# Merging three attention groups four heads at a time instead of eight

## The chip, the cores and the metric

The kernel runs on one core of a Trainium2 chip. The core has TensorE (PE in the profile: matrix multiply, with PEld for its weight loads), VectorE (DVE), ScalarE (ACT), GpSimd (POOL) and SyncE (SP), whose instruction stream issues all the transfers of this kernel. Each engine runs its own instructions in order, and engines wait for each other by semaphores. The metric is the device time of one execution in microseconds; of the kernel before there are three runs, 1656.64, 1657.37 and 1660.12 us.

## The reference

A trunk of two layers on 1024 tokens of width 1024. Layer A mixes tokens by dilated windowed attention, layer B by windowed attention with grouped keys. After each there is a residual layer norm and a gated addition. The part that matters here is in layer A: three groups of projections, each with its own window and dilation, and 16 heads of 64. Each group gives an output and a log-sum-exp per token and head, and the three are merged by a softmax over the groups:

```python
for gi, (window, dil) in enumerate(A_GROUPS):          # ((128, 1), (512, 4), (2048, 16))
    q, k, v = split_cols(h[..., base:base + 3 * A_WIDTH], [A_WIDTH] * 3)
    ...
    o, lse = banded_attention(strided(q)[:, :, :, None, :], strided(k), strided(v), window // dil)
    ...
wts = jax.nn.softmax(jnp.stack(lses, axis=0), axis=0)
o = jnp.einsum('gbsh,gbshd->bshd', wts, jnp.stack(outs, axis=0))
return (o * jax.nn.silu(z)) @ w_out
```

## The kernel before

Every projection is done with operands split into a high and a low half-precision part, so that one tile of 128 tokens by 512 columns is three matmuls for each of eight slices of the width, 24 in all (`lin`, L266 to L276). Weights come in blocks of 512 columns. A block is loaded in four transfers (`wraw`), its maximum is found by four VectorE reductions (L109), spread over the partitions by one small matmul on PE (`max_spread`, L237, which waits for VectorE's `mdd`), and it is split by ScalarE (L132) and VectorE (L133). These steps are handed out a few to a tile, ahead of the block's use.

Layer A (L623) runs over two pairs of four-head quarters (`pair`, and `q` from 0 to 3). For each pair and each group `g` in the order 1, 2, 0 there is a value stage of eight token tiles (v of the pair, L649 to L652) and two query/key stages (q and k of one quarter, L661 to L668). A query/key tile goes through the rotary step on VectorE (L347, L350), GpSimd (L351, L358) and ScalarE (L357, L361) and a transposing transfer (`qk`, L362). 1.67 tiles later (`UNIT_LAG`) an attention unit of four heads is due: scores on PE (L385), masked maximum on VectorE (L389), exponentials on ScalarE (L395), split of the weights (L399, L401), a transposing transfer (`pT`, L404); three units later the product with v on PE (L416 to L418), into one of two halves of a PSUM bank, which ScalarE empties into `st` (L698). `st` holds 256 output columns and 8 numbers for the denominators, and is stored to a DRAM tensor `scr` of its group (L707). Group 0 is the last, so when its tile is stored for both quarters of a pair, the three groups of that tile can be merged.

That is `merge`, a generator in three steps, which `merge_step` drives: at every third tile during most of the layer, at every tile from the second pair's group 0 on (`merge_every`). Step one loads the three groups from `scr` into `gt` (L749); step two computes the weights on VectorE with one exponential on ScalarE (L754 to L762) and starts the sum on GpSimd (L765 to L767); step three ends it on VectorE (L769, L770) and stores to `o_dr` (L771; `oa` in the profile). Two merges are under way at a time, in two buffers.

Behind layer A stands the gate projection `z`: eight tiles of its first half and one of the second in `z_block` (each through two ScalarE activations, L720 and L722, and VectorE's L723, and a store to `za`), the other seven in `mixed`. There each row tile's merged output `ot` and gate `og` are loaded, multiplied on GpSimd (L902), measured and split (L904, L263, L264) and transposed to `ogT`, from which the output projection reads (L920). One of its two weight blocks (`wo`) lies in a pool which is opened only when layer A's buffers are given back.

The source gives an order of creation, and a scheduler that models the engines in time moves instructions on each engine from it, so the order on an engine is read from the built program.

## Time and profile before

| what | value |
|---|---|
| median of three runs | 1657.37 us |
| the profiled execution | 1658.17 us, of which the span is 1656.4 us |
| PE busy | 1587.8 us, 96% of the span |
| VectorE, ScalarE, GpSimd busy | 1078.1, 922.7, 664.6 us |
| merges | 16, of eight heads and 128 tokens each |

The span is the time from the first to the last instruction that the profiler recorded on the core; the 1.8 us around it belong to the execution and are in no row. A busy PE is not yet PE at its peak, because the granted clock has two levels, 1.2 and 2.4 GHz, and a stage at the lower one is busy as well. The profile's column PEclk gives the mean of what was granted in a stretch as a share of 2.4 GHz. Idle time of another engine costs nothing as long as PE does not wait for it.

### The profile page before, as it was taken

The page shows a single profiled execution, that of the slowest core. Times are in us where ns is not written, and L with a number is a line of the kernel's source. Part 1 is how long each engine was busy: PE and PEld are TensorE (multiplying, and loading weights), DVE is VectorE, ACT ScalarE, POOL GpSimd, SP SyncE. Part 2 cuts the span into 40 slices and gives each one's busy share as a digit, 9 for nine tenths or more (in the row PEclk, how much of TensorE's full clock was granted, in tenths as well). Part 3 has the DMA queues.
Part 4 walks back from the last instruction along what each step waited for, and adds up shares of the span by engine and source line. Part 5 has one row for each costly group of instructions (what it writes and reads, how often), then busy time and mean ns, then how long its engine had stood idle before and what let it go on. Part 6 is the DMA issues. An engine that isn't in the chain of part 4 may idle for free. (4 is left out here: it accounts for less than half of the span.)

```text
span 1656.4 us, 29029 instructions
## 1 busy us (share of the span) xinstructions
PE 1587.8 (96%) x10579; PEld 883.2 (53%) x10579; DVE 1078.1 (65%) x2619; ACT 922.7 (56%) x2050; POOL 664.6 (40%) x477
## 2 busy tenths in 40 slices
PE   9999999999999799999999988899999998999998
PEld 3455676654555456666545543344455555544444
DVE  6866655655566776556466567887447998677731
ACT  4537665675774467656657843533334878754321
POOL 0015624532554665155235653453323452225341
PEclk9999999999999999999999998999999999999999
DMA  9718867775887777567658885989975898998963
GB/s 362 251 61 172 186 135 149 153 158 126 164 159 203 207 170 159 127 157 163 142 124 187 190 226 202 336 221 264 248 185 113 155 206 183 189 297 215 262 197 109
DMA packets 543792, 311.02 MB, mean 188 GB/s; under 512 B 473120, under 2 KB 494240, under 8 KB 543392
## 3 DMA queue, kind: packets, MB, share of 16 engines
q1 hardware_dynamic: 543648, 309.16, 75.3%
q8 instruction: 83, 1.36, 0.3%
q14 instruction: 61, 0.50, 0.1%
HBM read 137.78 MB, written 54.92 MB: 116 GB/s over the span
## 5 line engine op out<-in xcount | busy, mean ns | idle before, releaser
L272 PE MATMUL lin<-whl,xhl 128*128 128x512 f16 x1280 | 488.5, 382 | 2.6 <-ACT zu L722 2.6
L273 PE MATMUL lin<-whl,xhl 128*128 128x512 f16 x1280 | 488.7, 382 | 0.0
L274 PE MATMUL lin<-whl,xhl 128*128 128x512 f16 x1280 | 488.7, 382 | 0.0
L351 POOL TENSOR_TENSOR t<-t,t 128x512 f32<-128x512 f32 (+1 forms) x120 | 153.4, 1278 | 284.8 <-DVE t L350 268.0
L401 POOL TENSOR_TENSOR phl<-sm,phl 128x1024 f16<-128x1024 f32 (+1 forms) x88 | 155.6, 1769 | 233.3 <-ACT phl L399 205.9
L109 DVE TENSOR_REDUCE wpm<-wraw 128x1 f32<-128x1024 f32 (+1 forms) x132 | 156.8, 1197 | 93.6 <-DMA wraw<-in_wa_dram 54.8
L274 PEld LDWEIGHTS <-xhl 128*128 128x128 f16 x1280 | 149.3, 117 | 127.5 <-issue 3.5
L273 PEld LDWEIGHTS <-xhl 128*128 128x128 f16 x1280 | 149.7, 117 | 119.5 <-issue 6.7
L272 PEld LDWEIGHTS <-xhl 128*128 128x128 f16 x1280 | 149.4, 117 | 119.7 <-issue 3.8
L395 ACT ACTIVATE sm<-sm,st,cs 128x128 f32<-128x128 f32 (+1 forms) x384 | 203.6, 532 | 3.6 <-ACT st L393 0.4
L358 POOL TENSOR_TENSOR hl<-t,hl 128x512 f16<-128x512 f32 (+1 forms) x120 | 145.3, 1211 | 131.7 <-ACT hl L357 131.7
L389 DVE CUSTOM_DVE_ANT_0 sm<-s,tab 128x256 f32<-128x256 f32 (+1 forms) x512 | 157.0, 358 | 31.5 <-PE s L385 23.0
L133 DVE SCALAR_TENSOR_TENSOR whl<-wraw,s,whl 128x1024 f16<-128x1024 f32 (+1 forms) x116 | 168.3, 1501 | 12.8 <-ACT whl L132 12.8
L357 ACT ACTIVATE hl<-t 128x512 f16<-128x512 f32 (+1 forms) x120 | 72.3, 602 | 125.4 <-POOL t L351 124.0
L347 DVE TENSOR_TENSOR t<-lin,rope 128x512 f32<-128x512 f32 (+1 forms) x120 | 78.9, 657 | 75.7 <-PE lin L274 41.6
L132 ACT ACTIVATE whl<-wraw,s 128x1024 f16<-128x1024 f32 (+1 forms) x116 | 121.8, 1122 | 5.1 <-DVE s L212 5.0
L272 PE MATMUL lin<-whl,x2T 128*128 128x512 f16 (+1 forms) x320 | 115.5, 361 | 0.0
L273 PE MATMUL lin<-whl,x2T 128*128 128x512 f16 (+1 forms) x320 | 115.2, 360 | 0.0
L274 PE MATMUL lin<-whl,x2T 128*128 128x512 f16 (+1 forms) x320 | 115.0, 359 | 0.0
L399 ACT ACTIVATE phl<-sm 128x1024 f16<-128x1024 f32 (+1 forms) x128 | 110.2, 861 | 1.2
L361 ACT ACTIVATE hl<-hl 128x512 f16<-128x512 f16 (+1 forms) x104 | 63.2, 608 | 54.2 <-POOL hl L358 53.9
L385 PE MATMUL s<-qk 128*128 128x128 f16 x1120 | 81.5, 220 | 9.1 <-DMA qk<-hl 9.1
(187 smaller groups left out, 2883.5 us busy)
## 6 DMA issues: line engine op xcount, KB each, us to landing
wraw<-in_wa_dram SPq DMA_DIRECT2D x56, 512.0 KB, 6.0
scr<-st SPq DMA_DIRECT2D x96, 132.0 KB, 2.3
gt<-scr SPq DMA_DIRECT2D x48, 264.0 KB, 3.4
wraw<-in_wav_dram SPq DMA_DIRECT2D x24, 512.0 KB, 6.4
prh<-pro SPq DMA_DIRECT2D x32, 256.0 KB, 4.1
wraw<-in_wg_dram SPq DMA_DIRECT2D x16, 512.0 KB, 8.7
wraw<-in_wb_dram SPq DMA_DIRECT2D x16, 512.0 KB, 6.4
xg<-y SPq DMA_DIRECT2D x16, 512.0 KB, 3.6
```

The costliest lines, as they stand in the source:

```text
L109: k.nc.vector.tensor_reduce(pm[:, c:c + 1], self.raw[:, c * q:(c + 1) * q], axis=AX.X, op=ALU.max, apply_absolute_value=True)
L132: nc.scalar.activation(hl[:, 0, sl], self.raw[:, sl], AF.Copy, scale=self.s)
L133: self.last = nc.vector.scalar_tensor_tensor(hl[:, 1, sl], self.raw[:, sl], self.s, hl[:, 0, sl], op0=ALU.mult, op1=ALU.subtract)
L272: mm(ps, xh(kt), wh, start=(kt == 0), stop=False)
L273: mm(ps, xh(kt), wl, start=False, stop=False)
L274: mm(ps, xl(kt), wh, start=False, stop=(kt == NK - 1))
L351: nc.gpsimd.tensor_add(t1[:, :nh * HD], t1[:, :nh * HD], t2[:, :nh * HD])
L358: nc.gpsimd.tensor_sub(hl[:, :nh, HD:P], rv, hl[:, :nh, 0:HD])
L389: nc.vector.tensor_tensor_reduce(sm[:, h, :nk], ps[:, i, :nk], mask, 1.0, -3e38, ALU.add, ALU.max, mx[:, h:h + 1])
L395: nc.scalar.activation(sm[:, h, :nk], sm[:, h, :nk], AF.Exp, bias=nbias[:, h:h + 1], scale=cs, accum_out=sums[:, h:h + 1])
L399: nc.scalar.activation(hl[:, 0], sm[:, :, :nk], AF.Copy)
L401: eng.tensor_sub(hl[:, 1], sm[:, :, :nk], hl[:, 0])
```

## The change

A merge now covers one quarter, that is four heads, instead of a pair of quarters. It is created whenever a tile of group 0 is stored, for each `q`, and not only for the second of a pair. Its buffer `gt` holds half as many columns, there are three such buffers instead of two, and `merge_step` keeps up to three merges under way. All operations of a merge stay, on half as many elements; there are 32 merges.

```diff
-            if g == 0 and q % 2:
-                self.merges.append(self.merge(n, q // 2, scr[q // 2]))
+            if g == 0:
+                self.merges.append(self.merge(n, q, scr[q // 2]))
...
-    def merge(self, n, pair, scr):
+    def merge(self, n, q, scr):
...
-        gt = at.tile([P, 3, 2, 4 * HD + 8], F32, tag="gt", name="gt")
+        gt = at.tile([P, 3, 4 * HD + 8], F32, tag="gt", name="gt", bufs=3)
         for g in range(3):
-            nc.sync.dma_start(gt[:, g], scr[g][n * P:(n + 1) * P])
-        sums, nb = gt[:, :, :, 4 * HD:4 * HD + 4], gt[:, :, :, 4 * HD + 4:]
+            nc.sync.dma_start(gt[:, g], scr[g][n * P:(n + 1) * P, q % 2])
+        sums, nb = gt[:, :, 4 * HD:4 * HD + 4], gt[:, :, 4 * HD + 4:]
         yield
-        w = sp.tile([P, 3, 2, 4], F32, tag="mw", name="mw")
-        M = sp.tile([P, 2, 4], F32, tag="mM", name="mM")
...
+        w = sp.tile([P, 3, 4], F32, tag="mw", name="mw", bufs=3)
+        M = sp.tile([P, 4], F32, tag="mM", name="mM")
...
         nc.scalar.activation(w, w, AF.Exp)
...
         nc.gpsimd.tensor_mul(x[1], x[1], wb[1])
         nc.gpsimd.tensor_mul(x[2], x[2], wb[2])
         nc.gpsimd.tensor_add(x[1], x[1], x[2])
         yield
         nc.vector.tensor_mul(x[0], x[0], wb[0])
         nc.vector.tensor_add(x[0], x[0], x[1])
-        nc.sync.dma_start(self.o_dr[n][:, pair * 512:(pair + 1) * 512].rearrange("p (a c) -> p a c", a=2),
-                          gt[:, 0, :, 0:4 * HD])
+        nc.sync.dma_start(self.o_dr[n][:, 4 * HD * q:4 * HD * (q + 1)], gt[:, 0, 0:4 * HD])
...
-        while len(self.merging) < 2 and self.merges:
+        while len(self.merging) < 3 and self.merges:
```

The instructions move with it. VectorE, late in the z tiles, before: `zu` is a z tile (here the tenth and eleventh), `gt` belongs to the last two merges, `wpm` is the maximum of the first gate weight block.

```order
L109 TENSOR_REDUCE wpm_11795<-wraw_11693 128x1
L762 TENSOR_TENSOR mw_11620<-mw_11620,mL_11627 128x24
L723 SCALAR_TENSOR_TENSOR zu_11683<-zt_11681,zu_11683 128x512
L769 TENSOR_TENSOR gt_11610<-gt_11610,mw_11620 128x2x256
L109 TENSOR_REDUCE wpm_11795<-wraw_11693 128x1
L770 TENSOR_TENSOR gt_11559<-gt_11559 128x2x256
L109 TENSOR_REDUCE wpm_11795<-wraw_11693 128x1 x2
L239 TENSOR_REDUCE m2_11744<-s_11742 128x1
L770 TENSOR_TENSOR gt_11610<-gt_11610 128x2x256
L723 SCALAR_TENSOR_TENSOR zu_11728<-zt_11726,zu_11728 128x512
L218 TENSOR_REDUCE m1_11831<-wpm_11795 128x1
```

The same place on VectorE now, from the end of the last merge on (the first `zu` is the eighth z tile, the next the ninth and tenth):

```order
L769 TENSOR_TENSOR gt_11835<-gt_11835,mw_11881 128x256
L770 TENSOR_TENSOR gt_11835<-gt_11835 128x256
L723 SCALAR_TENSOR_TENSOR zu_11930<-zt_11928,zu_11930 128x512
L133 SCALAR_TENSOR_TENSOR whl_11970<-wraw_10759,s98_11899,whl_11970 128x1024 x4
L723 SCALAR_TENSOR_TENSOR zu_11966<-zt_11964,zu_11966 128x512
L109 TENSOR_REDUCE wpm_12131<-wraw_12029 128x1 x2
L723 SCALAR_TENSOR_TENSOR zu_12019<-zt_12017,zu_12019 128x512
L109 TENSOR_REDUCE wpm_12131<-wraw_12029 128x1 x2
L239 TENSOR_REDUCE m2_12080<-s_12078 128x1
L218 TENSOR_REDUCE m1_12167<-wpm_12131 128x1
```

The last merge operation (L770) stood between the tenth and the eleventh z tile, among the maxima (L109) of the next block; now it stands ahead of the eighth, and the split of a block (L133) and the maxima follow without a merge between them.

PE, where the output projection begins, before: L237 is the small matmul that spreads the maximum of the second gate weight block, `ogT` the first row tile.

```order
L274 MATMUL lin<-whl,xhl 128x512
L237 LDWEIGHTS ones
L237 MATMUL s<-mdd,ones 128x128
L272 LDWEIGHTS ogT
L272 MATMUL lin<-whl,ogT 128x512
L273 LDWEIGHTS ogT
```

The same matmul on PE now:

```order
L274 MATMUL lin<-whl,ogT 128x512
L237 LDWEIGHTS ones
L237 MATMUL s<-mdd,ones 128x128
L272 LDWEIGHTS ogT
L272 MATMUL lin<-wo,ogT 128x512
L273 LDWEIGHTS ogT
```

It stood between the last z tile and the first projection from `ogT`; now it stands 120 matmuls later, between the two halves of the third row tile.

SP's queue in the last query/key stage (second pair, group 0, `q` = 3), before. `scr0_1` to `scr2_1` are the three groups' stores of the second pair.

```order
L362 DMA_TRANSPOSE qk_10221<-hl_10227 128x12x128
L404 DMA_TRANSPOSE pT_10287<-phl_10284 128x16x128
L707 DMA scr0_1_618<-st_10050 128x264
L362 DMA_TRANSPOSE qk_10322<-hl_10328 128x12x128
L404 DMA_TRANSPOSE pT_10388<-phl_10385 128x16x128
L707 DMA scr0_1_618<-st_10154 128x264
L404 DMA_TRANSPOSE pT_10479<-phl_10476 128x8x128
L362 DMA_TRANSPOSE qk_10421<-hl_10427 128x12x128
L707 DMA scr0_1_618<-st_10254 128x264
```

The same stage on SP now, about the same transposes:

```order
L362 DMA_TRANSPOSE qk_10189<-hl_10195 128x12x128
L404 DMA_TRANSPOSE pT_10255<-phl_10252 128x16x128
L707 DMA scr0_1_618<-st_9998 128x264
L362 DMA_TRANSPOSE qk_10311<-hl_10317 128x12x128
L749 DMA gt_10400<-scr0_1_618 128x264
L771 DMA oa0_599<-gt_10152 128x256
L707 DMA scr0_1_618<-st_10100 128x264
L404 DMA_TRANSPOSE pT_10377<-phl_10374 128x16x128
L749 DMA gt_10521<-scr0_1_618 128x264
L749 DMA gt_10521<-scr1_1_619 128x264
L749 DMA gt_10521<-scr2_1_620 128x264
```

Between the transposes of `qk` and `pT` there are now three loads and a store of a merge to each tile. The exponentials of the first pair stood all in the value stage behind it and in the stage after that; now seven of the 16 stand in the query/key stage of `q` = 1. The second pair's eight for `q` = 2 stand in that of `q` = 3.

## Rows read from the trace of the kernel before

**Rows 1.** The page: busy us (share of the span) and instructions of each engine

```profile
PE 1587.8 (96%) x10579; PEld 883.2 (53%) x10579; DVE 1078.1 (65%) x2619; ACT 922.7 (56%) x2050; POOL 664.6 (40%) x477
```

**Rows 2.** Stage windows: stretch, length, busy us (count) per engine, PEclk, DMA share, GB/s

```profile
core 0: us, PE busy (x) PEld busy (x) DVE busy (x) ACT busy (x) POOL busy (x), PEclk, DMA share, GB/s
420.00:508.00 88.00, 88.00 (x715) 49.55 (x713) 57.22 (x141) 61.00 (x141) 47.39 (x31) 1.00 0.88 184
508.00:590.00 82.00, 69.79 (x505) 39.85 (x502) 61.62 (x151) 38.32 (x98) 52.49 (x38) 0.94 0.71 186
880.00:940.00 60.00, 59.06 (x553) 34.04 (x551) 36.64 (x102) 47.56 (x112) 35.30 (x25) 1.00 0.88 184
1013.00:1060.00 47.00, 31.95 (x121) 12.92 (x119) 37.07 (x73) 26.05 (x35) 16.38 (x12) 0.82 0.82 283
```

**Rows 3.** Timeline of PE, idle pieces: start, length, instruction, idle before and releaser

```profile
527.62 0.19 PE L416 MATMUL o<-vh,pT 128*128 128x64 f16 x1 [2.17 <-ACT st L698]
...
551.35 0.21 PE L416 MATMUL o<-vh,pT 128*128 128x64 f16 x1 [4.45 <-ACT st L698]
...
560.99 0.19 PE L416 MATMUL o<-vh,pT 128*128 128x64 f16 x1 [0.97 <-ACT st L698]
...
568.75 0.62 PE L385 MATMUL s<-qk 128*128 128x128 f16 x8 [1.50 <-DMA qk<-hl]
...
574.65 1.07 PE L385 MATMUL s<-qk 128*128 128x128 f16 x16 [3.12 <-DMA qk<-hl]
...
960.66 0.24 PE L416 MATMUL o<-vh,pT 128*128 128x64 f16 x1 [3.73 <-DMA pT<-phl]
...
1016.48 0.38 PE L272 MATMUL lin<-whl,xhl 128*128 128x512 f16 x1 [2.59 <-ACT zu L722]
...
1028.40 0.29 PE L237 MATMUL s<-mdd,ones 128*128 128x128 bf16 x1 [4.89 <-DVE mdd L230]
...
1054.14 0.29 PE L237 MATMUL s<-mdd,ones 128*128 128x128 bf16 x1 [7.33 <-DVE mdd L230]
```

**Rows 4.** Windows behind idle pieces, and one of ordinary z tiles; columns as above

```profile
1016.50:1020.10 3.60, 3.60 (x10) 1.28 (x10) 3.53 (x7) 1.19 (x2) 3.40 (x4) 0.53 0.78 315
1028.50:1034.00 5.50, 5.50 (x15) 2.03 (x15) 3.42 (x3) 4.60 (x5) 0.00 (x0) 0.52 0.75 236
1054.70:1057.70 3.00, 3.00 (x8) 1.07 (x9) 3.00 (x7) 2.44 (x4) 0.00 (x0) 0.50 0.93 228
529.70:531.90 2.20, 2.20 (x9) 0.80 (x7) 0.24 (x1) 2.20 (x9) 2.15 (x2) 0.50 1.30 118
552.60:556.00 3.40, 3.40 (x13) 1.19 (x11) 3.40 (x5) 0.00 (x0) 0.00 (x0) 0.51 0.08 28
990.00:1010.00 20.00, 20.00 (x95) 9.05 (x94) 13.99 (x31) 8.15 (x13) 8.08 (x6) 1.00 0.52 174
```

**Rows 5.** Waits: engine line <- releaser, us in total, times, longest

```profile
ACT mw L756 <- DVE mw L755: 24.3, 8, 8.5
...
ACT mw L756 <- DVE mw L755: 30.3, 6, 9.5
ACT wo L132 <- DMA oa<-gt: 10.7, 1, 10.7
...
DVE mM L754 <- DMA gt<-scr: 6.8, 2, 4.9
...
SPq L749 <- DMA scr<-st: 4.3, 4, 1.9
```

**Rows 6.** Tile `gt`: operations, ns min/median/max; then DMA issues of the page, KB, us

```profile
L758 DVE TENSOR_TENSOR mwl<-mw,gt x16: 170/182/1022, 511.7 to 1015.7; 128x24 f32<-128x24 f32 x16
L765 POOL TENSOR_TENSOR gt<-gt,mw x16: 1042/1548/1552, 512.6 to 1019.2; 128x512 f32<-128x512 f32 x16
L769 DVE TENSOR_TENSOR gt<-gt,mw x16: 691/692/1526, 514.6 to 1019.6; 128x512 f32<-128x512 f32 x16
...
scr<-st SPq DMA_DIRECT2D x96, 132.0 KB, 2.3
gt<-scr SPq DMA_DIRECT2D x48, 264.0 KB, 3.4
```

More of the change, by code (lines that the diff above doesn't have):

```diff
@@ L742, in z_block @@
                 self.w_z.released = True
-    def merge(self, n, pair, scr):
+    def merge(self, n, q, scr):
         nc, at, sp = self.nc, self.att, self.small
-        gt = at.tile([P, 3, 2, 4 * HD + 8], F32, tag="gt", name="gt")
+        gt = at.tile([P, 3, 4 * HD + 8], F32, tag="gt", name="gt", bufs=3)
         for g in range(3):
-            nc.sync.dma_start(gt[:, g], scr[g][n * P:(n + 1) * P])
-        sums, nb = gt[:, :, :, 4 * HD:4 * HD + 4], gt[:, :, :, 4 * HD + 4:]
+            nc.sync.dma_start(gt[:, g], scr[g][n * P:(n + 1) * P, q % 2])
+        sums, nb = gt[:, :, 4 * HD:4 * HD + 4], gt[:, :, 4 * HD + 4:]
         yield
-        w = sp.tile([P, 3, 2, 4], F32, tag="mw", name="mw")
-        M = sp.tile([P, 2, 4], F32, tag="mM", name="mM")
-        nc.vector.tensor_reduce(M, nb.rearrange("p g a h -> p a h g"), axis=AX.X, op=ALU.min)
-        nc.vector.tensor_sub(w, M.unsqueeze(1).to_broadcast([P, 3, 2, 4]), nb)
+        w = sp.tile([P, 3, 4], F32, tag="mw", name="mw", bufs=3)
+        M = sp.tile([P, 4], F32, tag="mM", name="mM")
+        nc.vector.tensor_reduce(M, nb.rearrange("p g h -> p h g"), axis=AX.X, op=ALU.min)
+        nc.vector.tensor_sub(w, M.unsqueeze(1).to_broadcast([P, 3, 4]), nb)
         nc.scalar.activation(w, w, AF.Exp)
-        wl = sp.tile([P, 3, 2, 4], F32, tag="mwl", name="mwl")
+        wl = sp.tile([P, 3, 4], F32, tag="mwl", name="mwl")
         nc.vector.tensor_mul(wl, w, sums)
-        L = sp.tile([P, 2, 4], F32, tag="mL", name="mL")
-        nc.vector.tensor_reduce(L, wl.rearrange("p g a h -> p a h g"), axis=AX.X, op=ALU.add)
+        L = sp.tile([P, 4], F32, tag="mL", name="mL")
+        nc.vector.tensor_reduce(L, wl.rearrange("p g h -> p h g"), axis=AX.X, op=ALU.add)
         nc.vector.reciprocal(L, L)
-        nc.vector.tensor_mul(w, w, L.unsqueeze(1).to_broadcast([P, 3, 2, 4]))
-        x = [gt[:, g, :, 0:4 * HD].rearrange("p a (h c) -> p a h c", c=HD) for g in range(3)]
-        wb = [w[:, g].unsqueeze(3).to_broadcast([P, 2, 4, HD]) for g in range(3)]
+        nc.vector.tensor_mul(w, w, L.unsqueeze(1).to_broadcast([P, 3, 4]))
+        x = [gt[:, g, 0:4 * HD].rearrange("p (h c) -> p h c", c=HD) for g in range(3)]
+        wb = [w[:, g].unsqueeze(2).to_broadcast([P, 4, HD]) for g in range(3)]
         nc.gpsimd.tensor_mul(x[1], x[1], wb[1])
```

## The prediction

> **What bounds the kernel now.** I read the busy line of the page first, then stage windows, then TensorE's idle time in order of time, then the clock behind each idle piece, then the waits of ScalarE, VectorE and the DMA queue. The busy line [rows 1] shows TensorE (PE) at 96% and no other engine above 65%: only time in which PE stands still, or runs slowly after it stood still, can be won. The stage windows [rows 2] say where that is. In the query/key stage before the first merges (420 to 508 us) PE works 88.00 of 88.00 us; in the next stage, where the eight merges of the first head pair run, 69.79 of 82; in the query/key stage of the second pair, which has no merges yet, 59.06 of 60; at the end of layer A, behind the last merges, 31.95 of 47.
>
> The idle pieces have names [rows 3]. Between 527 and 575 us there are five, 2.17 + 4.45 + 0.97 + 1.50 + 3.12 = 12.2 us; three wait for ScalarE's `st` (L698), which empties PE's output bank, two for a transpose of `qk`. At the end there are three: 2.59 (a z bank that ScalarE has not emptied), 4.89 and 7.33 (each a small matmul, L237, that spreads a weight block's maximum and waits for VectorE's `mdd`). Behind five of these pieces the granted clock is at the lower of its two levels, 0.50 to 0.53, for 2.2 to 5.5 us [rows 4]: 15 matmuls take 5.50 us there, against 95 in 20.00 us at 1.00. The loss is (1 - clock) x length: 1.7 + 2.6 + 1.5 = 5.8 us at the end, 1.1 + 1.7 = 2.8 us in the first merge stage.
>
> Who is late is in the waits [rows 5]. ScalarE runs its instructions in order, and a merge's exponential (L756) stands in that order wherever the scheduler put it. It waits for VectorE's subtraction, and this for the load of `gt`: 24.3 us in 8 waits in the first merge stage, 30.3 us in 6 at the end. Everything behind it waits too, `st` and the z tiles above all. VectorE itself waits for `gt` at the end (6.8 us in 2 waits), with the maxima of the next weight block queued behind it. And the second half of the output weights is split by ScalarE only when the last merge is stored, since it lies in the memory that the merge buffers leave: 10.7 us.
>
> So a merge costs PE nothing by its work but by standing in order before something. In the first stage that is (12.2 + 2.8) / 8 = 1.88 us for each merge; at the end 2.59 + 4.89 + 7.33 + 5.8 = 20.6 us in all.
>
> **The change part by part.** *What each merge does.* 16 merges of eight heads become 32 of four. The six small VectorE operations keep their length, about 0.18 us [rows 6], so 32 instead of 16 add 16 x 6 x 0.18 = 17 us to VectorE; the two large ones halve, 0.69 us each on 512 elements, and double in number, and so do GpSimd's three (1.55 us for L765). The loads go from 48 to 96. None of this is on PE's path by itself: in the stages that take it up VectorE would go from 36.6 of 60 us to some 52 and GpSimd from 35.3 to some 51 (eight half merges of about 1.9 us each) [rows 2]. If that cover were gone, the price would appear as waits, which the next terms bound.
>
> The Trainium skill speaks against this part: "VectorE: DVE Perf Modes", section on the TRN2 errata, says that operations on SBUF pay a fixed extra latency per instruction, so that small tiles pay it again and again. The trace agrees: 24 elements take 0.18 us, 512 take 0.69 [rows 6]. By the rule and by the rows the halves save less than half; the sum is the same by both, as VectorE is not the bound.
>
> *The end of layer A.* The second pair's first four heads are now merged in the query/key stage before, and only eight half merges are left for the z stage. On VectorE the last merge operation stood ahead of the eleventh z tile; now it stands ahead of the eighth. A z tile is 24 matmuls at 20.00/95 = 0.21 us [rows 4], 5.1 us, so the last merge is 15 us earlier against PE's work. ScalarE's wait for the last store (10.7 us), the `mdd` behind merge operations (4.89) and the z bank behind an exponential (2.59) have this cause: I take 2.59 + 4.89 + 1.7 + 2.6 = 11.8 us as won. The third piece, 7.33 + 1.5 = 8.8, waits for the last gate weight's `mdd`; the scheduler now puts that matmul five half tiles later, so PE next waits at most for `ogT`, whose rows can be loaded some 15 us earlier as well. I take 6 of 8.8, for what is late next is then the transpose. Term: -18; bounds -20.6 and -9 (half of the 11.8, a third of 8.8).
>
> *The first pair's merges.* Nine half merges still run where the eight whole ones ran (of 16 exponentials 7 stand ahead of that stage). What PE lost there, 15.0 us, goes; the nine cost something again. Bounds: nothing, as for the merges between 990 and 1010 us, beside which PE is busy 20.00 of 20.00 us [rows 4], and the full 1.88 each. I take half, 0.94, since a half merge holds its engines about half as long: 8.5. Term: -6.5; bounds -15.0 and +1.9.
>
> *The two query/key stages that take up merges.* 7 + 8 = 15 half merges come to stages that had none. Per merge the SP queue gets three loads, a store, and a wait for the `scr` store just before it (the trace has 4 such waits, 4.3 us, the longest 1.9 [rows 5]); behind it stand the transposes of `qk` and `pT`. On GpSimd and VectorE the rotary work stands behind merge operations, on ScalarE `st`. PE has no reserve to show in the second of these stages (59.06 of 60). Bounds: 0 and 1.88 each. I take 0.94, the same half: +14.1.
>
> *The z stage itself* keeps eight merges, halves for wholes, and I leave its piece of 3.73 at 960 us [rows 3] where it is: 0, bounds -3.7 and +4.
>
> **Sum.** The profiled execution took 1658.2 us (span 1656.4), the median of the runs shown is 1657.4. 1658.2 - 18 - 6.5 + 14.1 = 1647.8.
>
> **The rivals.**
>
> *A. The merges block the stages they come to (slower).* Place: the query/key stages, on SP, VectorE and GpSimd, which all run in order; there PE needs `qk` under two tiles after its projection, a tighter time than the value stage has. For it: the two pieces of 1.50 and 3.12 us are just this, merges among rotary work [rows 3]. Against it: a half merge holds GpSimd half as long. Price: the full 1.88 on each of 15, 28.2 us instead of 14.1: 1658.2 - 18 - 6.5 + 28.2 = 1661.9. It decides from 24.5 / 15 = 1.63 us per half merge.
>
> *B. The wait is for a transfer, and that does not halve (no change).* If what others wait for is the load's landing, a half merge costs by that. A 264 KB load lands in 3.4 us, a 132 KB transfer in 2.3 [rows 6]: 0.68 of 1.88 is 1.27. Nine cost 11.4 (term -3.6), fifteen 19.1: 1658.2 - 18 - 3.6 + 19.1 = 1655.7. For it: the exponential waits for the subtraction, and this for the load. Against it: three buffers instead of two, so loads can start a merge earlier. "DMA: Bandwidth & Descriptors" of the Trainium skill (Rules for kernel authors) would have many small transfers joined into one; the two rows agree that half the bytes do not take half the time.
>
> *C. The stages have room (faster than forecast).* The first of them runs at 88.00 of 88.00, lags of under two tiles and three units stand between producer and use, and the merges at 990 to 1010 us cost nothing. Then the fifteen are free: 1658.2 - 18 - 6.5 = 1633.7. Against it: the second stage is at 0.98 already.
>
> *D. The change does not do what it says.* With one step in three tiles the first pair's merges could be late all the same. Half true by the instruction order: nine of 16 stay in the value stage. It is in the sum.
>
> **How the numbers follow.** Forecast 1648: 0.45, its own range 1640 to 1655. A 0.21 (around 1662), B 0.17 (around 1656), C 0.17 (around 1634). Outside 1635 to 1663 lie half of C and nearly half of A, so that is the range of 8 in 10. About 0.2%, 3.3 us, can be told from no change. Faster: the forecast but 0.02, C, and a little of B: 0.61. Same: most of B, the near side of A: 0.18. Slower: 0.21.
>
> **What would show it.** Right: PE's pieces at the spread matmuls behind the z tiles gone or under 1 us, ScalarE's wait for `oa` gone, the clock at 1.00 through the z tiles; PE's loss in the first value stage about half; new small pieces, under 1 us a merge, in the two query/key stages. Wrong: the last stage still losing over 10 us with all merges done before (then the merges were not its cause), or PE pieces above 1.6 us a merge waiting for `qk` or `pT` at 430 to 505 and 890 to 945 us.

## The result: 0.9% slower, and where the time went

| | before | after |
|---|---|---|
| median | 1658.51 us (4 runs, 1656.64 to 1660.12) | 1673.11 us (4 runs, 1667.70 to 1674.62) |
| profiled execution | 1658.17 us, span 1656.4 | 1667.70 us, span 1665.9 |
| ratio | | 1.0091, 95% interval 1.0077 to 1.0104 |

The kernel became slower, by 14.6 us in the medians; the forecast was 10 us faster. The time also lies above the stated range, which ended at 1663. The profiled execution is the shortest of the four; a second profile of the same kernel, below, shows the same pattern, with larger losses.

The page's first row, busy time by engine, answers to [rows 1]: VectorE is busy for 38 us more, where 17 were counted, and GpSimd for 2.

```profile
PE 1588.1 (95%) x10579; PEld 883.6 (53%) x10579; DVE 1115.9 (67%) x2747; ACT 924.9 (56%) x2066; POOL 666.7 (40%) x525
```

Stage windows after the change, columns as in [rows 2]: in the two query/key stages, which ran at 88.00 of 88.00 and 59.06 of 60, PE now stands still for 7.0 and 5.6 us; in the stage behind the first of them, 508 to 590 us, it still does for 9.9 of 82. In the z tiles between 1018 and 1038 us PE works without a pause at full clock.

```profile
420.00:508.00 88.00, 80.99 (x628) 45.05 (x627) 67.44 (x173) 57.08 (x133) 58.50 (x51) 0.96 0.89 187
508.00:590.00 82.00, 72.14 (x540) 41.63 (x539) 62.22 (x175) 39.91 (x103) 38.83 (x40) 0.98 0.70 176
880.00:940.00 60.00, 54.39 (x472) 31.08 (x470) 47.46 (x128) 40.53 (x101) 37.81 (x34) 0.97 0.96 202
...
1018.00:1038.00 20.00, 20.00 (x96) 9.14 (x95) 13.42 (x20) 6.82 (x8) 3.46 (x2) 1.00 0.89 294
```

PE's idle pieces, from its timeline, answer to [rows 3]. The first four are new and stand in the two query/key stages. Of the three at the end of layer A (2.59, 4.89, 7.33) one of 2.16 is left. The last three are in the output projection, where before the change only one piece was above 2 us; it is shown behind them.

```profile
477.81 0.21 PE L416 MATMUL o<-vh,pT 128*128 128x64 f16 x1 [3.08 <-ACT st L698]
500.41 0.19 PE L416 MATMUL o<-vh,pT 128*128 128x64 f16 x1 [3.80 <-ACT st L698]
...
924.82 0.23 PE L416 MATMUL o<-vh,pT 128*128 128x64 f16 x1 [5.05 <-DMA pT<-phl]
...
958.77 0.21 PE L416 MATMUL o<-vh,pT 128*128 128x64 f16 x1 [2.81 <-ACT st L698]
...
1048.84 0.38 PE L272 MATMUL lin<-whl,xhl 128*128 128x512 f16 x1 [2.16 <-ACT zu L722]
...
1107.12 0.38 PE L272 MATMUL lin<-wo,ogT 128*128 128x512 f16 x1 [2.46 <-DVE y L920]
1116.85 0.61 PE L272 MATMUL lin<-whl,ogT 128*128 128x512 f16 x1 [4.33 <-DMA ogT<-rhl]
...
1132.39 0.39 PE L272 MATMUL lin<-whl,ogT 128*128 128x512 f16 x1 [2.12 <-DMA ogT<-rhl]
```

Before the change, in the projection:

```profile
1111.59 0.39 PE L272 MATMUL lin<-whl,ogT 128*128 128x512 f16 x1 [3.07 <-DMA ogT<-rhl]
```

Idle pieces don't add up to a difference by themselves, since the clock falls behind some of them. So I followed one matmul through both traces: line L272 runs 2120 times in each kernel, and the same start in PE's timeline, counted from 0, stands for the same place in the program. The lag of after against before at such places is worked out in this table, and its growth is what a stretch costs.

| matmul of L272 | place | before, us | after, us | lag |
|---|---|---|---|---|
| 512 | ahead of the first merges | 433.7 | 433.7 | 0.0 |
| 592 | two tiles behind the first pair's last query/key projection | 495.9 | 506.5 | +10.6 |
| 848 | the first pair's merges are over | 707.2 | 712.2 | +5.0 |
| 1104 | where the second pair's begin | 895.7 | 900.6 | +4.9 |
| 1168 | two tiles behind the second pair's last query/key projection | 950.2 | 969.5 | +19.3 |
| 1232 | in the z tiles | 1003.3 | 1020.5 | +17.2 |
| 1280 | start of the output projection | 1054.7 | 1054.0 | -0.7 |
| 1440 | first gate tiles | 1168.2 | 1177.3 | +9.1 |
| 2112 | end | 1649.4 | 1658.6 | +9.2 |

The first pair costs 5.0 us more (10.6 in the query/key stage, 5.6 of it regained in the stage behind), the second 12.2 (17.2 - 4.9, in unrounded numbers; 14.4 in the query/key stage, up to matmul 1168, and 2.1 of it regained in the z tiles). The end of layer A gives back 17.9, and the output projection takes 9.8 again. Layer B changes nothing.

Waits in the query/key stages of after answer to [rows 5]; the first three lines are from 466 to 520 us, the last is SP's queue from 905 to 960. PE waits for `st`, ScalarE for a merge's subtraction, VectorE for its load; in the later stage the transposes of the attention weights stand behind GpSimd's merge operations, which were not there before.

```profile
PE o L416 <- ACT st L698: 6.9, 2, 3.8
...
ACT mw L756 <- DVE mw L755: 9.1, 5, 2.3
...
DVE mM L754 <- DMA gt<-scr: 4.9, 3, 2.3
...
SPq L404 <- POOL gt L767: 10.0, 5, 3.1
```

What half a merge costs its engines is in the operations on tile `gt`, against [rows 6]. The three numbers are the shortest, the median and the longest in ns: the median of L769 goes from 692 to 425, of GpSimd's L765 from 1548 to 850, of a small operation from 182 to 170.

```profile
L758 DVE TENSOR_TENSOR mwl<-mw,gt x32: 155/170/2104, 442.5 to 1012.0; 128x12 f32<-128x12 f32 x32
L769 DVE TENSOR_TENSOR gt<-gt,mw x32: 412/425/1490, 445.4 to 1012.9; 128x256 f32<-128x256 f32 x32
L765 POOL TENSOR_TENSOR gt<-gt,mw x32: 608/850/853, 445.4 to 1012.9; 128x256 f32<-128x256 f32 x32
```

And from the page's DMA issues: half the load takes 2.6 us to land where the whole one takes 3.4.

```profile
scr<-st SPq DMA_DIRECT2D x96, 132.0 KB, 2.4
gt<-scr SPq DMA_DIRECT2D x96, 132.0 KB, 2.6
```

### The profile page after: what moved, and what is told of

It is laid out like the page before. It is cut to its first block, busy times and chain, and to the rows that moved or that the text cites. A ratio compares the mean times of both kernels' runs of the same rounds, so it can differ in the third digit from the quotient of the medians.

```text
span 1665.9 us, 29328 instructions
## 1 busy us (share of the span) xinstructions
PE 1588.1 (95%) x10579; PEld 883.6 (53%) x10579; DVE 1115.9 (67%) x2747; ACT 924.9 (56%) x2066; POOL 666.7 (40%) x525
## 5 line engine op out<-in xcount | busy, mean ns | idle before, releaser
L272 PE MATMUL lin<-whl,xhl 128*128 128x512 f16 x1280 | 487.8, 381 | 2.2 <-ACT zu L722 2.2
L274 PE MATMUL lin<-whl,xhl 128*128 128x512 f16 x1280 | 487.2, 381 | 0.0
L351 POOL TENSOR_TENSOR t<-t,t 128x512 f32<-128x512 f32 (+1 forms) x120 | 153.7, 1280 | 292.0 <-DVE t L350 266.1
L274 PEld LDWEIGHTS <-xhl 128*128 128x128 f16 x1280 | 149.1, 117 | 127.0 <-issue 2.9
L109 DVE TENSOR_REDUCE wpm<-wraw 128x1 f32<-128x1024 f32 (+1 forms) x132 | 156.8, 1196 | 85.7 <-DMA wraw<-in_wa_dram 47.5
L272 PEld LDWEIGHTS <-xhl 128*128 128x128 f16 x1280 | 149.3, 117 | 118.9 <-issue 2.2
L358 POOL TENSOR_TENSOR hl<-t,hl 128x512 f16<-128x512 f32 (+1 forms) x120 | 141.9, 1183 | 112.5 <-ACT hl L357 111.8
L133 DVE SCALAR_TENSOR_TENSOR whl<-wraw,s,whl 128x1024 f16<-128x1024 f32 (+1 forms) x116 | 163.6, 1459 | 8.6 <-ACT whl L132 8.6
L274 PE MATMUL lin<-whl,x2T 128*128 128x512 f16 (+1 forms) x320 | 114.8, 359 | 0.0
L272 PE MATMUL lin<-whl,x2T 128*128 128x512 f16 (+1 forms) x320 | 114.7, 359 | 0.0
L393 ACT ACTIVATE st<-mx,ncs 128x4 f32<-128x4 f32 x96 | 28.1, 292 | 115.8 <-DVE mx L389 91.4
```

The source lines that it names most:

```text
L109: k.nc.vector.tensor_reduce(pm[:, c:c + 1], self.raw[:, c * q:(c + 1) * q], axis=AX.X, op=ALU.max, apply_absolute_value=True)
L133: self.last = nc.vector.scalar_tensor_tensor(hl[:, 1, sl], self.raw[:, sl], self.s, hl[:, 0, sl], op0=ALU.mult, op1=ALU.subtract)
L272: mm(ps, xh(kt), wh, start=(kt == 0), stop=False)
L274: mm(ps, xl(kt), wh, start=False, stop=(kt == NK - 1))
L351: nc.gpsimd.tensor_add(t1[:, :nh * HD], t1[:, :nh * HD], t2[:, :nh * HD])
L358: nc.gpsimd.tensor_sub(hl[:, :nh, HD:P], rv, hl[:, :nh, 0:HD])
```

## The experiments

All runs in one table. The four columns behind the ratio are the growth of the lag against before, as above, in the profiled execution: first pair (512 to 848), second pair (1104 to 1232), end of layer A (1232 to 1280), output projection (1280 to 1440). Each is one profile. The two profiles of the changed kernel differ by up to 2.3 us in a column, so I read nothing into less. What the columns leave out is at most 2.9 us ahead of the first matmul, 2.6 from there to 512, 0.7 between 848 and 1104 and 3.1 behind 1440, but for the runs with old data, without loads and with rows six ahead, where it is told below.

| run | median, us | ratio to before, 95% | first | second | end of A | projection |
|---|---|---|---|---|---|---|
| changed kernel | 1673.11 | 1.0077 to 1.0104 | 5.0 | 12.2 | -17.9 | 9.8 |
| the same again | 1677.00 | 1.0098 to 1.0136 | 5.6 | 14.5 | -17.2 | 11.2 |
| halves, taken up late | 1683.14 | 1.0130 to 1.0180 | 4.2 | 0.9 | +6.4 | 9.8 |
| first pair late | 1676.76 | 1.0097 to 1.0134 | 6.1 | 12.7 | -12.9 | 9.1 |
| no exponential | 1672.61 | 1.0071 to 1.0116 | 7.5 | 12.2 | -19.8 | 10.3 |
| one step of lag | 1672.44 | 1.0068 to 1.0102 | 7.1 | 8.4 | -14.8 | 7.8 |
| short maxima | 1673.76 | 1.0074 to 1.0111 | 6.7 | 12.0 | -13.9 | 6.0 |
| no GpSimd work | 1676.28 | 1.0090 to 1.0126 | 8.6 | 15.3 | -19.8 | 10.5 |
| old data | 1680.88 | 1.0112 to 1.0160 | -3.3 | 0.4 | -20.2 | 7.8 |
| transfers alone | 1653.32 | 0.9961 to 0.9990 | -8.7 | 8.0 | -19.2 | 10.3 |
| work without loads | 1671.51 | 1.0046 to 1.0096 | -16.9 | -2.7 | -20.2 | 7.2 |
| spread early | 1674.84 | 1.0066 to 1.0120 | 5.4 | 13.9 | -14.9 | 7.8 |
| spread in row 0 | 1680.01 | 1.0095 to 1.0140 | 5.5 | 12.0 | -15.2 | 10.5 |
| rows six ahead | 1680.70 | 1.0101 to 1.0162 | 5.7 | 11.8 | -15.1 | 7.1 |
| before, spread late | 1661.35 | 1.0000 to 1.0028 | 1.1 | -0.8 | -5.4 | 5.8 |
| two tiles, second pair | 1666.64 | 1.0031 to 1.0079 | -1.8 | 10.0 | -12.4 | 8.5 |
| two tiles, both pairs | 1669.85 | 1.0045 to 1.0086 | 0.7 | 10.9 | -12.3 | 9.9 |

**The changed kernel again.** No edit.

> The changed kernel once more, on the chip on which the other runs of this group are timed. Its four times so far were 1667.7 to 1674.6 us, the profiled one the shortest. If there is a second pattern of waits in its longer executions, this profile may show it: then the time is 1672 to 1675 and some stage loses 5 us more than in the first profile. If not, 1667 to 1669 with the same stages: 11 us lost in the query/key stage of the first pair, 12 in that of the second, 18 won behind the last merge, 10 given back in the output projection.

It is 1.2% slower than before on this chip, and no other stage appears: the same four columns, 7.6 us more at matmul 2112, of it 2.3 in the second pair, 1.4 in the projection and 2.3 behind it.

**Halving or place, first pair.** Halves are taken up only when the pair is complete. The edit is shown; a further run does the same for the first pair alone:

```diff
-            if g == 0:
-                self.merges.append(self.merge(n, q, scr[q // 2]))
+            if g == 0 and q % 2:
+                self.merges.append(self.merge(n, q - 1, scr[q // 2]))
+                self.merges.append(self.merge(n, q, scr[q // 2]))
```

> Half merges, three under way, but the halves of a pair are taken up only when the pair's third group is complete, as before the change. Theory P (the place costs): the query/key stages lose nothing again, the first value stage loses about 15 us and the end of layer A about 20, as before the change; time within 4 us of the kernel before, 1654 to 1662. Rival H (halving itself costs, each half as much as a whole merge): the value stage behind the first pair loses 25 to 30 us, and the time is 1670 or more.

> The first pair's halves are taken up only when the pair is complete, the second pair's as in the changed kernel. Theory P: the 11 us lost in the first query/key stage go, the value stage behind it loses 15 instead of some 7; net -3, so about 3 us below the changed kernel, and 12 us are still lost in the second pair's query/key stage. If a half merge costs as much wherever it stands (rival F, a fixed price of 1.5 us): the 16 halves lose 24 us in the value stage and what follows, and the time is 3 to 6 us above the changed kernel.

Late or early, 16 halves lose the first pair 4 to 6 us more than eight whole merges did. Those lost 15.0 [rows 3, 4], so by estimate a half costs (15.0 + 5) / 16 = 1.25 us. In the second pair late halves cost nothing in the query/key stage and 6.4 more at the end, where the output projection now waits for the last merged row, in PE's timeline of that run:

```profile
1068.13 0.58 PE L272 MATMUL lin<-whl,ogT 128*128 128x512 f16 x1 [18.11 <-ACT ot L904]
```

**Place without halving.** The kernel before, but a merge covers two tiles of one quarter, so it is taken up early and keeps its size, its two buffers and its loads (it has two stores for one); first for the second pair alone, then for both:

```diff
-            if g == 0 and q % 2:
-                self.merges.append(self.merge(n, q // 2, scr[q // 2]))
+            if g == 0 and n % 2:
+                self.merges.append(self.merge(n - 1, q // 2, scr[q // 2], q))
...
-            nc.sync.dma_start(gt[:, g], scr[g][n * P:(n + 1) * P])
+            nc.sync.dma_start(gt[:, g], scr[g][n * P:(n + 1) * P] if q is None else
+                              scr[g][n * P:(n + 2) * P, q % 2].rearrange("(a p) c -> p a c", p=P))
```

> The first pair's merges as before the change; those of the second pair taken up early as in the change, but of eight heads' size: two tiles of one quarter each, two under way. So the second pair's place is changed and no merge is halved. Theory H (halving is what costs: a half merge loses 1.25 us in the first pair where a whole one loses 1.88): the first pair loses as before (15 us), the query/key stage of the second some 8 us (four merges at 1.88), 18 us or more are won behind the last merge; with 10 us given back in the output projection the time is 1655 to 1660. Theory P (the place costs 12 us there whatever the size): 1660 to 1664.

> Both pairs' merges of two tiles of one quarter each: early as in the change, no merge halved. Theory H: eight merges of the first pair lose 15 us as before the change, wherever they stand, and the time is that of the run with two tiles in the second pair alone, within 3 us. Theory P (a query/key stage is the worse place): 5 us or more above it.

The first pair loses what it lost before (0.7 and -1.8), early or not: there halving was the price. The second pair loses 10.0 and 10.9 us although no merge is halved: there the place is the larger part. The halves' 12.2 and 14.5 lie 1 to 5 us above that, too little beside 2.3 of noise to say what halving adds there. The two theories had 8 and 12 us for this stage, and the runs lie between them. The end of layer A gives back only 12.4, where 18 were expected, so the time of the first run, 1666.64 us, is above both forecasts, and the second run, 3.2 us above the first, falls between theirs. Neither kernel beats the one before.

**What in a merge costs the query/key stages.** One thing left out or eased at a time in the changed kernel: the exponential; GpSimd's three operations; the part just stored (a merge loads group 1 twice); a step more between load and use, with four buffers and four merges under way:

```diff
-        nc.scalar.activation(w, w, AF.Exp)
```
```diff
-        nc.gpsimd.tensor_mul(x[1], x[1], wb[1])
-        nc.gpsimd.tensor_mul(x[2], x[2], wb[2])
-        nc.gpsimd.tensor_add(x[1], x[1], x[2])
```
```diff
-            nc.sync.dma_start(gt[:, g], scr[g][n * P:(n + 1) * P, q % 2])
+            nc.sync.dma_start(gt[:, g], scr[g or 1][n * P:(n + 1) * P, q % 2])
```
```diff
-        gt = at.tile([P, 3, 4 * HD + 8], F32, tag="gt", name="gt", bufs=3)
+        gt = at.tile([P, 3, 4 * HD + 8], F32, tag="gt", name="gt", bufs=4)
...
         yield
+        yield
```

> The changed kernel without the exponential of the merges on ScalarE (the differences serve as weights; nothing else is left out). Theory S (ScalarE stands in order behind a merge's load): the waits for st go, the two query/key stages lose under 6 us together instead of 23, the time is 1640 to 1650. Rival L (the loads on SP's queue and the work on VectorE and GpSimd delay the transposes): the stages still lose 15 us or more, by waits for qk and pT, and the time is 1660 to 1668.

> The changed kernel without GpSimd's three operations in each merge (groups 1 and 2 are left out of the sum; VectorE's operations, ScalarE's and the transfers stay). Theory G (GpSimd, busy 16.9 of 20 us in the first of these stages, delays the rotary work and the split of the attention weights, and by the memory port it shares with VectorE slows that engine as well: 1.21 us for a 128x12 product that takes 0.17 alone): the two query/key stages lose under 8 us together instead of 22, the time is 12 us or more below the changed kernel. Rival W (waits for loads): the stages lose 14 us or more, and the time is 0 to 8 us below it.

> The changed kernel, but a merge loads group 1's part twice, and not the part of group 0 that has just been stored (group 0 is left out; as many bytes and operations). Theory W (a load stands behind the fresh store on SP's queue, and lands late): the two query/key stages lose under 10 us together instead of 22, and the time is 10 us or more below the changed kernel. Rivals C and G (the work itself): they lose 16 us or more, and the time is within 5 us of it.

> The changed kernel with four half merges under way in four buffers and one more step between a merge's loads and their first use. Theory W (VectorE reaches a merge before its loads have landed, and what stands behind it on VectorE, GpSimd and ScalarE waits too; VectorE waits 4.9 us for loads in the first query/key stage, 4.0 in the second): these waits go, the two query/key stages lose 10 us or less together instead of 22, and the time is 8 to 14 us below the changed kernel. Rival C (the work itself, a merge's operations among the rotary work on GpSimd and VectorE, which slow each other): the stages lose 18 us or more, and the time is within 4 us of the changed kernel.

Neither the exponential nor GpSimd's work nor the short lag is the cause alone: the first pair loses as much or more, the second 12.2 and 15.3 us, and 8.4 with the longer lag, the one gain. That gain lies behind the query/key stage: up to matmul 1168 the run with the longer lag loses 13.8 us, the changed kernel 14.4. Without the exponential the waits move: between 466 and 520 us ScalarE now waits for the attention maxima on VectorE, and GpSimd for the merge's weights.

```profile
ACT st L393 <- DVE mx L389: 14.7, 4, 4.7
...
POOL gt L764 <- DVE mw L761: 9.4, 6, 4.0
```

The run with old data says less than hoped: without the wait for a store the scheduler put merges a stage earlier. From the first matmul to matmul 512 it lost 12.4 us, and between 848 and 1104 another 18.2. Merges cost there too, without fresh data; whether fresh data are part of the price in the query/key stages, it doesn't tell.

**Transfers alone, and work without loads.** All operations out, three loads and a store stay; then the loads out (three buffers of ones):

```diff
-        w = sp.tile([P, 3, 4], F32, tag="mw", name="mw", bufs=3)
...
-        nc.vector.tensor_add(x[0], x[0], x[1])
```
```diff
-        gt = at.tile([P, 3, 4 * HD + 8], F32, tag="gt", name="gt", bufs=3)
-        for g in range(3):
-            nc.sync.dma_start(gt[:, g], scr[g][n * P:(n + 1) * P, q % 2])
+        gt = self.gts[0]
+        self.gts = self.gts[1:] + [gt]
```

> The changed kernel with the merges' transfers alone: three loads and a store each, no operation on VectorE, ScalarE or GpSimd (group 0 is stored unmerged). Theory K (the operations, standing in order on three engines, delay the rotary work and the attention weights): the query/key stages lose under 6 us together instead of 22. Theory Q (the transfers do, on SP's queue and the DMA engines, which are busy 86 to 97% of the time there): they lose 14 us or more.

> The changed kernel without the merges' loads: they work in three buffers filled with ones at the start, all operations and the stores stay (the sum is left out with that). Theory K: the query/key stages lose 14 us or more together. Theory Q: 8 us or less, since 48 of the 64 transfers of a pair's merges are gone. If both the operations and the wait for their loads are needed, some 5 to 12 us here and under 6 in the run with transfers alone.

The operations are the larger part of the price in the first pair: without them it is 8.7 us better than before the change, and 13.7 better than in the changed kernel, of the 20 us that its 16 halves cost. In the second pair the transfers alone lose 8.0 us, against 12.2 with the operations, by waits for transposes (PE's idle pieces in that run):

```profile
916.05 0.20 PE L416 MATMUL o<-vh,pT 128*128 128x64 f16 x1 [3.94 <-DMA pT<-phl]
...
953.70 1.89 PE L385 MATMUL s<-qk 128*128 128x128 f16 x16 [4.50 <-DMA qk<-hl]
```

The run without loads says nothing about the two query/key stages: with nothing to wait for, all 32 merges were scheduled far ahead, the last store of a merge at 268 us, and from the first matmul to matmul 512 the run lost 40.1 us, or 1.25 a half merge. It does confirm two readings of the kernel before: with no merge left behind matmul 512 the first pair is 16.9 us better than before the change and the end of layer A 20.2, where the rows gave 15.0 and 20.6.

**The output projection.** It takes 6 to 11 us more in every run with early or halved merges, even with transfers alone, where it starts 20 us earlier, and with late halves, where it starts 13 us later. Three suspects: VectorE, which after the change is busy there for 85.84 of 100.80 us; the moved spread matmul, which stands 120 matmuls behind the first of the projection in all of these runs but the two that move it back; and the rows' own preparation. First VectorE, with maxima over 64 columns in five blocks; then the second gate block's preparation ahead of the first row, or within it; then rows prepared six ahead of their use and not four:

```diff
-pm[:, c:c + 1], self.raw[:, c * q:(c + 1) * q]
+pm[:, c:c + 1], self.raw[:, c * q:c * q + (64 if 22 <= k.blocks.index(self) <= 26 else q)]
```
```diff
+        self.prepare(11 if l == 0 else 0)
         for n in range(NT):
             norm(n)
```
```diff
-                self.prepare(W_OP)
+                self.prepare(W_OP if l or n else 6)
```
```diff
-ROWS_AHEAD = 4
+ROWS_AHEAD = 6
```

> The changed kernel, but the maxima of five weight blocks around the first output projection (two gate blocks, three blocks of layer B) are taken over 64 columns of each 1024 or 512, so VectorE has some 15 us less to do between 1065 and 1130 us, where it works without a pause (that part of the maxima is left out). Theory V (the output projection runs at VectorE's pace): of the 10 us lost there 5 or more go, the time is 5 to 10 us below the changed kernel. Rival T (it runs at the pace of the row loads and transposes on SP's queue): it still loses 8 us or more, and the time is within 3 us of the changed kernel.

> The changed kernel with the preparation of the second gate block (maxima, spread matmul L237, split) written ahead of the output projection's first row, so that on PE its spread matmul stands where it stood before the change, 120 matmuls earlier than in the changed kernel; nothing else on PE moves ahead of it. Theory M (the matmul that was moved back holds up the split of that block on ScalarE and VectorE, which then falls into the output projection, with the load that waits for the freed weight buffer behind it): of the 10 to 11 us that the output projection loses against before, 5 or more go, less a wait of up to 2 us for mdd; the time is 4 to 9 us below the changed kernel. Rival R (the projection runs at the pace of the row loads, products and transposes, whatever VectorE does): it still loses 8 us or more, the time is within 3 us of the changed kernel.

> The same preparation written within the first row of the output projection, the spread matmul one row (48 matmuls and more) later than in the run before it in this group and 72 earlier than in the changed kernel. Theory M: half of the gain of that run or more, without its wait for mdd: 3 to 8 us below the changed kernel. Rival R: within 3 us of it.

> The changed kernel with the rows of the output projection prepared six ahead of their use instead of four. Theory R (the rows' own chain of loads, product, split and transpose sets the pace of the output projection): of the 10 us given back there 5 or more go, the time is 5 us or more below the changed kernel. Theory M (VectorE with the weight blocks' work): within 3 us of it.

None brings the time back. With short maxima the projection loses 6.0, but the end of layer A gives back only 13.9. With the spread matmul in its old place it loses 7.8, and from the first matmul on `ogT` to the first on `xgT` it still takes 100.6 us, although VectorE is busy for 77.6 of them, as before the change (the windows below). So the amount of VectorE's work isn't what makes the projection long; its order may be. PE waits there for a transposed row:

```profile
1117.93 0.61 PE L272 MATMUL lin<-whl,ogT 128*128 128x512 f16 x1 [10.60 <-DMA ogT<-rhl]
```

With rows six ahead the same window is 96.0 us, the shortest of the runs with early or halved merges, but the run loses 11.7 us behind matmul 1440.

The opposite was clearer: the kernel before, with the spread matmul where the change puts it.

```diff
-        e = k.max_spread(diag)
+        with k.tc.issue_after(k.last_mm.ins) if k.blocks.index(self) == 23 else nullcontext(): e = k.max_spread(diag)
```

> The kernel before the change, with one thing of the changed kernel: the spread matmul of the second gate block (L237) stands 120 matmuls later on PE, where the change puts it. Its wait of 7.33 us ahead of the output projection goes, and 1.5 us at the lower clock with it. If this wait was on the path of the end (as the prediction had it), 6 to 9 us are won: 1648 to 1652. Theory M or R (VectorE, ScalarE and the rows' transposes set the pace of the output projection, and the wait was time in which they got ahead): what is won there is lost again within the output projection, and the time is within 3 us of the kernel before.

1661.35 us, ratio 1.0014 (1.0000 to 1.0028): nothing won. PE's idle pieces there (in this kernel L280 stands for L272 to L274): instead of 7.33 us for `mdd` it waits 6.18 for the first transposed row, and then 3.82 and 5.80 within the projection.

```profile
1049.44 3.15 PE L280 MATMUL lin<-whl,ogT 128*128 128x512 f16 x7 [6.18 <-DMA ogT<-rhl]
...
1107.69 7.04 PE L280 MATMUL lin<-whl,ogT 128*128 128x512 f16 x24 [3.82 <-DMA ogT<-rhl]
1125.76 4.54 PE L280 MATMUL lin<-whl,ogT 128*128 128x512 f16 x13 [5.80 <-DVE rt L1010]
```

Windows from the first matmul on `ogT` to the first on `xgT`, columns as in [rows 2], for before, after and this run: 92.3, 100.8 and 98.7 us. The move alone makes the projection 6.4 us longer, and it starts 5.3 us earlier.

```profile
1054.70:1147.00 92.30, 86.78 (x386) 38.25 (x387) 77.24 (x159) 32.12 (x36) 41.45 (x23) 0.97 0.95 255
```
```profile
1054.00:1154.80 100.80, 88.73 (x388) 38.80 (x388) 85.84 (x169) 38.47 (x44) 40.15 (x24) 0.95 0.89 237
```
```profile
1049.40:1148.10 98.70, 89.02 (x388) 39.08 (x389) 82.65 (x167) 36.46 (x41) 42.70 (x24) 0.93 0.92 239
```

VectorE's busy time in the window goes from 77 us to 86 and 83. The split of the block (`wg`) lies in the window in all three, with 8.5, 7.3 and 6.7 us, so it is no part of that growth, which is spread over many operations. What changed is where in the window it stands. VectorE's timeline before the change: `mdd` is made at 1053.80, its spread read (L239) at 1054.47, the split follows from 1061 on, and at 1070.96 SP can load the next block into the freed buffer.

```profile
1053.80 0.29 DVE L230 TENSOR_SCALAR mdd<-tab,mde 128x128 bf16<-128x128 f32 x1
1054.47 0.29 DVE L239 TENSOR_REDUCE m<-s 128x1 f32<-128x128 f32 x1 [0.38 <-PE s L237]
...
1064.36 6.05 DVE L133 SCALAR_TENSOR_TENSOR wg<-wraw,s,wg 128x1024 f16<-128x1024 f32 x3
...
1070.96 1.42 SPq L102 DMA_DIRECT2D wraw<-in_wb_dram  x3
```

After it: `mdd` is ready at 1056.12, nearly as early, but the matmul stands behind 120 others, so L239 reads at 1092.37, and the split lies among the sums of the rows (L920); the load comes 32 us later.

```profile
1056.12 0.29 DVE L230 TENSOR_SCALAR mdd<-tab,mde 128x128 bf16<-128x128 f32 x1
...
1092.37 0.28 DVE L239 TENSOR_REDUCE m<-s 128x1 f32<-128x128 f32 x1
...
1094.97 3.64 DVE L133 SCALAR_TENSOR_TENSOR wg<-wraw,s,wg 128x1024 f16<-128x1024 f32 x2 [1.29 <-ACT wg L132]
1098.53 0.74 DVE L920 SCALAR_TENSOR_TENSOR y<-lin,osc,y 128x512 f32<-128x512 f32 x1
1099.19 3.48 DVE L133 SCALAR_TENSOR_TENSOR wg<-wraw,s,wg 128x1024 f16<-128x1024 f32 x2
...
1102.70 1.28 SPq L102 DMA_DIRECT2D wraw<-in_wb_dram  x3
```

## Why the prediction was wrong, step by step

**What bounds the kernel:** right. PE's stalls and the lower clock behind them decide, and the loss is in them.

**The end of layer A, -18:** 17.9 up to the start of the output projection. That the number is met so closely is partly luck: of the 11.8 us taken as won a piece of 2.16 for a z bank stayed, and of the 8.8 behind it, at that place, nothing was left. (The 30.3 us of ScalarE's waits "at the end" reach back to 960 us; behind 1000 us they are 10.5 in 2 waits. No term used them.) The failed step is the sentence that behind the third piece "PE next waits at most for `ogT`", from which 6 of 8.8 us were taken as won. The matmul that was moved back had work behind it: a split on two engines, a freed buffer, a load. In the kernel before, moving it alone won 5.3 us at the start and lost 6.4 in the projection. That wait was not on the path of the end. That VectorE and the rows got ahead during it is argued from the timelines; the runs show the exchange alone. In the changed kernel the projection lost 9.8 by matmuls, and 8.5 by the window in which the move alone cost 6.4. But putting the matmul back did not undo the loss there, so how much of it is the move stays open.

**The first pair's merges, -6.5:** near. 5.6 us were regained behind matmul 592.

**The two query/key stages, +14.1:** mis-sized. 10.6 + 12.2 = 22.8 us for 15 half merges, 1.52 each where 0.94 was taken; with the second pair read at matmul 1168, the place that answers to 592, it is 25.0 and 1.67 each, and the 2.1 regained behind it belong to the z stage, which was put at 0. "A half merge holds its engines about half as long" is what failed: by medians GpSimd's product takes 0.55 of the time, VectorE's 0.61, a small operation 0.93, the load 0.76. And the medians hide that the small operations with two inputs got longer by their mean, not shorter (last section). In the first pair a half costs 1.25 of 1.88, or 0.67. That this is the price of rival B (0.68, from the transfers) is chance, since in that pair 13.7 of the 20 us go when the transfers stay and the operations are left out. In the second pair merges of full size lose 10.0 and 10.9 us, so most of the loss there comes with their place.

**The sum** with the measured terms: 1658.2 - 17.9 - 5.6 + 22.8 + 9.8 = 1667.3, against 1667.7 profiled.

**The rivals.** A had the sign, and its stages: the measured 1.52 to 1.67 lies about its deciding 1.63; with 9.8 us in the projection, which no case had, it was enough. B's 1.27 a half is below it. C falls with the idle pieces. Of the signs of being right, the spread matmuls' pieces and the wait for `oa` are gone, and that was not enough, since no sign was named for the stage behind. The first value stage still lost 9.4 of its 15.0 us, a little more than the half that was named. The signs for the query/key stages counted idle pieces alone: these are 6.9 us for seven half merges up to 505 us and 9.9 for eight from 905 to 960, about the 1 us a merge that was named for right, and only 5.05 of them wait for `pT`, none for `qk`. So neither sign showed the 10.6 and 14.4 us that the lag shows.

Not settled: what in a merge holds up the query/key stages. The exponential and GpSimd's work are each not it alone. In the second pair the transfers suffice for 8.0 us; in the first it is mostly operations, and no run leaves out VectorE's small ones by themselves, which are the obvious suspect that remains.

## What to carry to other kernels

Before a stall is booked as won, follow what the stalled instruction releases, through the other engines and buffers to the next stage: a wait may cost nothing because others use the time, and moving the waiting instruction back moves its successors too (here 5.3 us won and 6.4 lost). Work that is halved in size and doubled in number should be priced from rows of both sizes, and where it is moved into a stage that runs at 98%, at the dearer bound until a run shows otherwise. Change place and size in separate runs: here the first pair paid for the size, the second mostly for the place.

## What was not expected of the hardware

A small VectorE operation can take as long as the GpSimd instruction beside it. The changed kernel's timeline in the first query/key stage, VectorE and then GpSimd:

```profile
476.06 0.17 DVE L754 TENSOR_REDUCE mM<-gt 128x4 f32<-128x12 f32 x1 [1.60 <-DMA gt<-scr]
476.26 0.89 DVE L755 TENSOR_TENSOR mw<-mM,gt 128x12 f32<-128x12 f32 x1
477.07 0.41 DVE L770 TENSOR_TENSOR gt<-gt 128x256 f32<-128x256 f32 x1
477.43 1.21 DVE L758 TENSOR_TENSOR mwl<-mw,gt 128x12 f32<-128x12 f32 x1
...
475.01 2.12 POOL L401 TENSOR_TENSOR phl<-sm,phl 128x1024 f16<-128x1024 f32 x1
477.09 1.52 POOL L351 TENSOR_TENSOR t<-t,t 128x512 f32<-128x512 f32 x1
```

L755 and L758, on 12 elements, take 0.89 and 1.21 us where the median of L758 is 0.17, and they end at 477.15 and 478.64, with GpSimd's instructions (477.13 and 478.61); the longest L758 took 2.10 us. The Trainium skill, "SBUF — State Buffer", section "SBUF: two separate sides", has the rule: a VectorE operation with two inputs from SBUF and a GpSimd instruction that reads SBUF exclude each other for the whole instruction. The two rows agree.

They are not alone. A merge has three such small operations with two inputs, L755, L758 and L762, 96 in the changed kernel. Of these, 30 take over 0.25 us, and each of the 30 ends 0.02 to 0.04 us after a GpSimd instruction. Their sums over the kernel (after the bar: busy us, mean ns):

```profile
L758 DVE TENSOR_TENSOR mwl<-mw,gt 128x12 f32<-128x12 f32 x32 | 15.9, 496 | 4.6 <-ACT mw L756 4.4
L755 DVE TENSOR_TENSOR mw<-mM,gt 128x12 f32<-128x12 f32 x32 | 14.4, 451 | 0.6
L762 DVE TENSOR_TENSOR mw<-mw,mL 128x12 f32<-128x12 f32 x32 | 12.6, 394 | 0.7
```

Together they take 42.9 us, where 48 of them took 12.6 before; at their medians it would be 16.4 and 8.8. That is most of the 38 us by which VectorE's busy time grew where 17 were counted: the prediction priced them at a median, 0.18 us, but the mean is 0.45 now and was 0.26. So many small operations are dear in stages where GpSimd works. Whether this is what holds up the query/key stages is not shown: without the merges' own GpSimd work, but with the rotary work there, the three operations still took 33.5 us, and the two pairs lost 8.6 and 15.3.
